# Splitting the expert weights in pieces of 2048 columns, with six landing places instead of nine

## The chip, the cores and the metric

One core of a Trainium2 chip runs the whole program: TensorE (PE; PEld is its weight load), VectorE (DVE), ScalarE (ACT), GpSimd (POOL), and the queue on SyncE (SP) that issues the loads from HBM. The metric is the device time of one execution in microseconds, lower is better.

## The reference

A transformer with two blocks on 256 tokens of width 1024, all in fp32. The first block has a mixer (mLSTM and gMLP), a cross-attention, and a mixture of experts; the second has two layers of a convolution, linear attention and pooling mixer with a gated feed-forward. The part that matters here is the mixture of experts, which comes after a router that gives every token two of 32 experts:

```python
def expert_block(args):
    xb, e = args
    return (jax.nn.silu(xb @ w_gate[e]) * (xb @ w_up[e])) @ w_down[e]
```

With d = 1024 and 512 hidden columns an expert has three matrices of 2 MB each, so 32 experts have 192 MB of weights, all of which are read once.

## The kernel before

**Splits.** A matmul at full precision is made of faster ones: a weight tile `raw` is split in a high part `whi` (a copy on ACT that rounds, line 455) and a low part `wlo` (`raw - whi` on DVE, line 456), and PE multiplies with both. A split of 1024 columns is called a chunk; `wlo` of a chunk needs its `whi`. In the expert stage a chunk feeds four matmuls of 512 columns (lines 968 and 969 for gate and up, 985 and 986 for down), which alternate between `whi` and `wlo`.

**The expert stage.** Experts go in 16 pairs; `up(j)` computes gate and up of pair j from 16 chunks, `down(j)` the down projection from 8. Pairs 13 and 14 are finished late: there is no down between `up(14)` and `up(15)`. Each chunk is a step; small work stands in `plan[step]`, and a generator that yields n goes on n steps later. Of that small work: `features` gathers a pair's tokens (PE, then ACT writes `XT`, line 876), `gate` and `gated` form silu(gate) times up (`z`, `g`; lines 900 to 910), `fold` transposes the result (PE line 925, which reads `g`) and writes `at`, `combine` adds results into the token sums (line 944), and `filters` prepares tables of the second block (lines 1303 to 1325). On PE, ACT and DVE the order is exactly the order in which this code runs (`manual_schedule`), each engine in order.

**Rings and landing places.** Weights of this stage are loaded 1 MB at a time (two chunks) by SP into landing places that are taken in turn: `EARLY` = 2 tiles of their own and seven tiles of the first block that have become free (`PLACES`). `load()` is called after the second chunk of a place is split, and SP issues that load when both parts have been read out of the place it reuses. `whi` has a ring of `NH` = 5 chunks and `wlo` one of `NL` = 4; `weights()` splits ahead:

```python
self.pos += 1
self.ahead(min(self.pos - 1 + NH, self.most))
```

So with chunk n the splits of chunk n+4 stand in the program. Its `whi` reuses the buffer of chunk n-1 and its `wlo` that of chunk n, and ACT or DVE waits until PE has finished there.

**Elsewhere.** Outside of the expert stage the same `whi` and `wlo` rings are filled chunk by chunk (512 KB loads, line 273), in an order that the scheduler chooses. Between the router and the stage stands a branch (`beyond`, a loop for overflowing experts, run zero times), at which all engines meet.

Of the kernel before, what the change touches and what calls it, by code (L numbers as in the profile page):

```python
# [31 lines left out]
P = 128  # L32
D = 1024
# [34 lines left out]
def _cols(v):  # L68
# [15 lines left out]

WHEN = dict(features=((0, 7), (0, 10), (0, 12), (0, 15), (1, 15), (1, 17), (1, 19), (1, 21)), chosen=0,
            weighted=(0, 3, 6, 9), filters=((4, 18), (8, 23)), combine=(3, 5, 7, 9), mask=8, fold=1)

# [163 lines left out]
class Kernel:  # L251
    def __init__(self, nc, tc, ins, out):
        self.nc, self.tc, self.ins, self.out = nc, tc, ins, out
        self.stream, self.loads, self.splits, self.pos, self.streaming = [], 0, 0, 0, False
        self.first_block = True
        self.raws, self.ready = deque(), deque()


# [6 lines left out]
    def weights(self, name, n, parts=None):  # L265

        if self.streaming:
            self.pos += 1
            self.ahead(min(self.pos - 1 + NH, self.most))
            return self.ready.popleft()  # L270
        w = min(1024, self.ins[name].shape[2])
        raw = self.raw(w)
        self.nc.sync.dma_start(raw, self.ins[name][n // 2][:, n % 2 * 1024:][:, :w])
        if self.first_block:
            with self.tc.high_priority(200):
                return self.parts(raw)
        return self.parts(raw, parts)

    def parts(self, raw, parts=None):
        hi, lo = parts or (None, None)  # L280
        hi = self.whi.tile([P, 1024], F32R, name="whi") if hi is None else hi
        lo = self.wlo.tile([P, 1024], F32R, name="wlo") if lo is None else lo
        self.split(hi, lo, raw)
        return hi, lo

    def load(self):

        if self.loads < len(self.stream):
            name, n = self.stream[self.loads]
            if name == "w_v0" and n == 0:  # L290
                self.gains = [self.bcast(g, pool=self.experts, tag="XT", bufs=6) for g in ("g_final", "norm_mix_pre0")]
# [3 lines left out]
            self.raws.append(raw)  # L295
            self.nc.sync.dma_start(raw, self.ins[name][n])
# [82 lines left out]

    def bcast(self, name, row=0, n=D, pool=None, tag="gbc", bufs=None):  # L380
        a = self.ins[name]
        t = (pool or self.gbc).tile([P, n], F32, name="gbc", tag=tag, bufs=bufs)
        self.nc.sync.dma_start(t, bass.AP(tensor=a.tensor, offset=a.offset + row * n, ap=[[0, P], [1, n]]))
        return t
# [113 lines left out]
    def block1(self, outer, moe):  # L498
# [3 lines left out]
        with ExitStack() as ctx:  # L502
# [216 lines left out]
            early = moe.enter_context(tc.tile_pool(name="early", bufs=1, reuse_waits="tile"))  # L719
            self.places = deque([(early, f"early{n}") for n in range(EARLY)] + [(outer, tag) for tag in PLACES])  # L720
            for j in range(PAIRS + 1):
# [3 lines left out]
                for d in DOWN(j):  # L725
                    self.stream.extend(("w_ed", 4 * d + 2 * m + n) for n in range(2) for m in range(2))
            self.most = 2 * len(self.stream) + 2
            self.stream.extend(("w_v0", n) for n in range(2))
# [72 lines left out]
            normed = []  # L801
            self.dense_n(oT, "w_o_x", 0, 8, residual(0))
            self.dense_n(oT, "w_o_x", 1, 8, residual(1, logits), True)
            for t in range(2):
                self.route(a, L[:, t], A[:, t], W[:, t])
# [7 lines left out]
    def moe(self, hh, hl, A, W):  # L813
# [4 lines left out]
        with ExitStack() as ctx:  # L818
# [59 lines left out]

            def weighted(o, t, h):


                if t == h == 0:
                    DT[o] = self.junk.tile([P, 4, S], F32, name="DT", tag="xn", bufs=2)
                Dw = a.tile([P, 2, 2, SLOTS], F32, name="Dw")
                for n in range(2):
                    j = 4 * o + 2 * h + n
                    nc.vector.tensor_scalar(Dw[:, n], self.c["slot"][:, None, :].to_broadcast([P, 2, SLOTS]),
                                            rp[:, t, j:j + 1], wp[:, t, j:j + 1], op0=OP.is_equal, op1=OP.mult)
                yield 4
                ps = self.tp()  # L890
                for n in range(2):
                    nc.tensor.transpose(ps[:, n * P:(n + 1) * P], Dw[:, n].rearrange("p i j -> p (i j)"), self.ident)
                yield 2
                nc.scalar.activation(DT[o][:, 2 * h:2 * h + 2, t * P:(t + 1) * P],
                                     ps[:, :2 * P].rearrange("p (n s) -> p n s", s=P), AF.Copy)

            def gate(j, p):
                yield 3
                z = a.tile([SLOTS, 512], F32, name="z")
                nc.scalar.activation(z, p[SLOTS:], AF.Copy)  # L900
                yield 1
                nc.vector.tensor_add(z, p[:SLOTS], z)
# [5 lines left out]
            def gated(j, p):  # L908
                yield 2
                nc.vector.tensor_mul(G[j], G[j], p)  # L910
# [8 lines left out]
            def fold(j, steps):  # L919
# [12 lines left out]
                yield 1  # L932
                nc.vector.tensor_sub(at[:, :, 1], pt, at[:, :, 0].bitcast(F32))

            def result(j, n, p):
                yield 2
                Y[j, n] = a.tile([P, 512], F32, name="ye", bufs=2)
                nc.scalar.activation(Y[j, n], p, AF.Copy)
# [61 lines left out]
            for k in range(2):  # L1000
                start(features(0, k))
            self.ahead(2)
            go_on()
            for j in range(PAIRS + 1):
# [9 lines left out]
                if j == PAIRS - 1:  # L1014
                    plan[22].append(fold(j, 3))
                if j == 1 or j % 4 == 3 and j < PAIRS - 1:
# [30 lines left out]
            xg = [self.junk.tile([P, D], F32, name="xn", bufs=2) for t in range(2)]  # L1047
            ws = [a.tile([P, 2, 512], F32, name="w", tag="at", bufs=2) for t in range(2)]
            ws = [[w[:, n] for n in range(2)] for w in ws]
# [33 lines left out]
            for t in range(2):  # L1083
                next(combine(PAIRS - 1, t, 1))
            with tc.manual_schedule(engines=engines - {mybir.EngineType.PE}):
                tiles = [chain(half(t, 0), half(t, 1)) for t in range(2)]
                for step in ORDER:
                    if step < 2:
                        next(tiles[step])
                    elif step == 3:  # L1090
                        next(spectra[1])
                    else:
                        self.ahead(self.splits + 1)
            self.streaming = False
            return hT

    def rank(self, a, hh, hl, A, W, rk, mine):
# [31 lines left out]
        self.ahead(2)  # L1129
        self.beyond(a, hh, hl, trips, late)  # L1130
# [227 lines left out]
    def mix(self, l, hT):  # L1358
# [3 lines left out]
        with ExitStack() as ctx:  # L1362
# [75 lines left out]
            nc.sync.dma_start(raw, self.ins[f"w_lr{l}"][0])  # L1438
            wlr = self.whi.tile([P, 1024], F32R, name="whi")
            nc.scalar.activation(wlr, raw, AF.Copy)  # L1440
# [265 lines left out]
```

## Time and profile before

| | us |
|---|---|
| median of 3 runs (lowest, highest) | 1703.29 (1701.62, 1704.55) |
| the profiled execution: its own time | 1706.44 |
| its span, first to last instruction | 1704.6 |
| expert stage in it, first to last matmul of the experts | 262.9 to 801 |

The times of the trace are counted from the start of the span. The span and the time of the profiled execution differ by 1.8 us, which lie around the instructions.

### The profile page before, as it was taken

How to read it: one execution, taken by the hardware profiler on the slowest of the kernel's cores; microseconds unless marked ns; L12 is line 12 of the kernel's file. 1: busy time of each engine (PE TensorE's matmuls, PEld its weight loads, DVE VectorE, ACT ScalarE, POOL GpSimd, SP SyncE). 2: the span in 40 equal slices, each digit the busy share in tenths (PEclk: the TensorE clock that was granted, in tenths of full speed). 3: DMA queues.
4: the chain of work that ended last, by engine and by line, in shares of the span. 5: the costliest groups of instructions: out<-in, count | busy, mean ns of one | idle time of the engine just before them, and what ended most of it. 6: DMA issues, size and time to landing. Idle time of an engine off the chain costs nothing. (4 is left out here: it accounts for less than half of the span.)

```text
span 1704.6 us, 24749 instructions
## 1 busy us (share of the span) xinstructions
PE 1635.3 (96%) x9115; PEld 1380.2 (81%) x9115; DVE 1288.6 (76%) x1702; ACT 1133.9 (67%) x1576; POOL 30.3 (2%) x47
## 2 busy tenths in 40 slices
PE   7999987999999999988999999999999999999998
PEld 6897875777767777766799887999878998789986
DVE  7876566999989999998569667677556886667763
ACT  7765437899878899986667545555445864555552
POOL 1000000000000000000000000000000000000000
PEclk9999998999999999999999999999999999999999
DMA  8546537999999999994775356455756545635561
GB/s 292 199 155 204 191 148 266 352 380 373 381 380 380 402 386 408 416 400 170 253 252 186 128 189 223 143 185 182 238 171 222 202 150 181 214 130 185 183 198 62
DMA packets 94448, 415.92 MB, mean 244 GB/s; under 512 B 12324, under 2 KB 18868, under 8 KB 68468
## 3 DMA queue, kind: packets, MB, share of 16 engines
q1 hardware_dynamic: 89220, 405.91, 65.6%
q0 software_dynamic: 864, 6.29, 1.0%
q10 hardware_dynamic: 4240, 2.10, 0.4%
q8 instruction: 73, 1.20, 0.3%
q14 instruction: 51, 0.42, 0.1%
HBM read 411.12 MB, written 3.15 MB: 243 GB/s over the span
## 5 line engine op out<-in xcount | busy, mean ns | idle before, releaser
L456 DVE TENSOR_TENSOR wlo<-raw,whi 128x1024 fp32r<-128x1024 f32 x709 | 844.3, 1220 | 210.7 <-PE acc L333 80.7
L455 ACT ACTIVATE whi<-raw 128x1024 fp32r<-128x1024 f32 x711 | 728.7, 1055 | 230.6 <-PE acc L334 116.7
L337 PE MATMUL acc<-hl,whi 128*128 128x256 f32 x1024 | 289.9, 283 | 0.0
L338 PE MATMUL acc<-hh,wlo 128*128 128x256 f32 x1024 | 289.9, 283 | 0.0
L336 PE MATMUL acc<-hh,whi 128*128 128x256 f32 x1024 | 289.7, 283 | 0.0
L968 PE MATMUL misc<-whi,XT 128*128 128x512 f32 x512 | 227.5, 444 | 1.1 <-ACT XT L876 1.1
L969 PE MATMUL misc<-wlo,XT 128*128 128x512 f32 x512 | 208.5, 407 | 5.2 <-DVE wlo L456 5.1
L336 PEld LDWEIGHTS acc<-hh,whi 128*128 128x128 f32 x1024 | 196.5, 192 | 0.1
L337 PEld LDWEIGHTS acc<-hl,whi 128*128 128x128 f32 x1024 | 196.5, 192 | 0.0
L338 PEld LDWEIGHTS acc<-hh,wlo 128*128 128x128 f32 x1024 | 196.5, 192 | 0.0
L969 PEld LDWEIGHTS misc<-wlo,XT 128*128 128x128 f32 x512 | 97.9, 191 | 47.7 <-DVE wlo L456 22.4
L968 PEld LDWEIGHTS misc<-whi,XT 128*128 128x128 f32 x512 | 98.1, 192 | 30.4 <-issue 8.9
L332 PE MATMUL acc<-whi,hh 128*128 128x512 f32 x288 | 113.3, 395 | 0.6 <-ACT hh L423 0.5
L333 PE MATMUL acc<-wlo,hh 128*128 128x512 f32 x288 | 113.0, 393 | 0.1
L334 PE MATMUL acc<-whi,hl 128*128 128x512 f32 x288 | 112.4, 391 | 0.0
L985 PE MATMUL misc<-whi,at 128*128 128x512 f32 x256 | 105.8, 413 | 4.3 <-ACT whi L455 2.2
L986 PE MATMUL misc<-wlo,at 128*128 128x512 f32 x256 | 104.1, 407 | 1.7 <-DVE wlo L456 1.7
L944 PE MATMUL acc<-ye,DT 128*128 128x512 f32 x128 | 65.3, 595 | 0.0
L986 PEld LDWEIGHTS misc<-wlo,at 128*128 128x128 f32 x256 | 48.1, 188 | 20.7 <-DVE wlo L456 9.9
L332 PEld LDWEIGHTS acc<-whi,hh 128*128 128x128 f32 x288 | 54.3, 189 | 12.8 <-ACT hh L423 1.2
L334 PEld LDWEIGHTS acc<-whi,hl 128*128 128x128 f32 x288 | 54.2, 188 | 11.6 <-DVE hl L424 0.7
L333 PEld LDWEIGHTS acc<-wlo,hh 128*128 128x128 f32 x288 | 54.4, 189 | 11.3 <-DVE wlo L456 0.5
(466 smaller groups left out, 2724.0 us busy)
## 6 DMA issues: line engine op xcount, KB each, us to landing
raw<-in_w_egu SPq DMA_DIRECT2D x128, 1024.0 KB
raw<-in_w_ed SPq DMA_DIRECT2D x64, 1024.0 KB
raw<-in_w_up SPq DMA_DIRECT2D x80, 512.0 KB
raw<-in_w_gate SPq DMA_DIRECT2D x48, 512.0 KB
raw<-in_w_down SPq DMA_DIRECT2D x44, 512.0 KB
raw<-in_w_qk SPq DMA_DIRECT2D x24, 512.0 KB
raw<-in_w_out SPq DMA_DIRECT2D x24, 512.0 KB
raw<-in_w_br SPq DMA_DIRECT2D x24, 512.0 KB
```

What stands on the lines that cost most here:

```text
L332: mm(out, xh, wh, start=start, stop=False)
L333: mm(out, xh, wl, start=False, stop=False)
L334: mm(out, xl, wh, start=False, stop=stop)
L336: mm(out, wh, xh, start=start, stop=False)
L337: mm(out, wh, xl, start=False, stop=False)
L338: mm(out, wl, xh, start=False, stop=stop)
L455: self.nc.scalar.activation(hi, src, AF.Copy)
L456: self.nc.vector.tensor_sub(lo, src, hi.bitcast(F32))
L968: mm(p, l, wh[:, c], start=s == k == 0, stop=False)
L969: mm(p, l, wl[:, c], start=False, stop=s == 7 and k == 1)
L985: mm(p, l, wh[:, c], start=s == k == 0, stop=False)
L986: mm(p, l, wl[:, c], start=False, stop=s == 3 and k == 1)
```

## The change

The expert stage splits a whole landing place with one instruction on ACT and one on DVE (2048 columns; the last place of the stream in two halves). The rings have four buffers of two chunks each for the high and four for the low part: three `whi` and two `wlo` tiles, and one respectively two tiles of the first block (`hTh`; `hTl`, `mTh`), which are landing places no more. Six places are left. With each even chunk n the split of the place three places further stands in the program. Outside of the stage a tile of the ring holds two chunks (`half`), so a new tile waits for both chunks of the old one. The gains of the last norm are loaded into a landing place, one `at` buffer lies in an `XT` one, the sixth place is loaded earlier, and the step counts of the small work are other ones.

```diff
-NB, NH, NL = 6, 5, 4
-PLACES = ("kT", "qk", "mTl", "y", "hTh", "hTl", "mTh")
+NB, NH, NL = 6, 3, 2
+PLACES = ("kT", "qk", "mTl", "y")
 EARLY = 2
+HIS, LOS = ("whi", "whi", "whi", "hTh"), ("wlo", "wlo", "hTl", "mTh")
-WHEN = dict(features=((0, 7), (0, 10), (0, 12), (0, 15), (1, 15), ...
-            weighted=(0, 3, 6, 9), filters=((4, 18), (8, 23)), ...
+WHEN = dict(features=((0, 9), (0, 11), (0, 13), (0, 15), (1, 15), ...
+            weighted=(0, 2, 4, 6), filters=((5, 19), (13, 23)), ...
...
         if self.streaming:
+            if self.pos % 2 == 0:
+                self.ahead(min(self.pos // 2 + len(HIS), self.pos + 2))
             self.pos += 1
-            self.ahead(min(self.pos - 1 + NH, self.most))
             return self.ready.popleft()
...
+    def half(self, n):
+        if not self.halves[n]:
+            t = (self.whi, self.wlo)[n].tile([P, 2048], F32R, name=("whi", "wlo")[n])
+            self.halves[n] = [t[:, 1024:], t[:, :1024]]
+        return self.halves[n].pop()
...
-        hi = self.whi.tile([P, 1024], F32R, name="whi") if hi is None else hi
-        lo = self.wlo.tile([P, 1024], F32R, name="wlo") if lo is None else lo
+        hi = self.half(0) if hi is None else hi
+        lo = self.half(1) if lo is None else lo
...
     def ahead(self, n):
-        while self.splits < min(n, 2 * len(self.stream)):
-            raw = self.raws[0]
-            self.ready.append(self.parts(raw[:, self.splits % 2 * 1024:][:, :1024]))
-            self.splits += 1
-            if self.splits % 2 == 0:
-                self.raws.popleft()
-                self.load()
+        while self.splits < min(n, len(self.stream) - 2):
+            for _ in self.apart(2048):
+                pass
+    def apart(self, w):
+        raw = self.raws.popleft()
+        self.splits += 1
+        hi, lo = (ring[0][0].tile([P, 2048], F32R, name="part", tag=ring[0][1]) for ring in self.rings)
+        for ring in self.rings:
+            ring.rotate(-1)
+        for a in range(0, 2048, w):
+            c = slice(a, a + w)
+            self.split(hi[:, c], lo[:, c], raw[:, c])
+            self.ready.extend((hi[:, b:b + 1024], lo[:, b:b + 1024]) for b in range(a, a + w, 1024))
+            if a + w < 2048:
+                yield
+        self.load()
...
             self.dense_n(oT, "w_o_x", 0, 8, residual(0))
+            self.load()
             self.dense_n(oT, "w_o_x", 1, 8, residual(1, logits), True)
...
-                yield 1 if q == 0 else 2
+                yield 1
                 nc.scalar.activation(XT[q][k // 2][:, k % 2]...
...
             def gated(j, p):
-                yield 2
+                yield 1
                 nc.vector.tensor_mul(G[j], G[j], p)
...
-                AT[j] = a.tile([P, 4, 2, 2, SLOTS], F32R, name="at", bufs=2)
+                AT[j] = a.tile([P, 4, 2, 2, SLOTS], F32R, name="at", **(dict(tag="XT", bufs=6) if j == PAIRS - 2 else {}))
```

The first place is DVE's order from the `z` of pair 14, in the middle of `up(14)`, to the `at` of that pair in `up(15)`. Before:

```order
L902 TENSOR_TENSOR z<-misc,z 64x512
L456 TENSOR_TENSOR wlo<-raw,whi 128x1024 x6
L910 TENSOR_TENSOR g<-g,misc 128x512
L456 TENSOR_TENSOR wlo<-raw,whi 128x1024 x4
L933 TENSOR_TENSOR at<-tp,at 128x8x64
```

Now (line 481 is the low split, which writes a `part`; the high one is line 480):

```order
L932 TENSOR_TENSOR z<-misc,z 64x512
L481 TENSOR_TENSOR part<-raw,part 128x2048 x2
L940 TENSOR_TENSOR g<-g,misc 128x512
L481 TENSOR_TENSOR part<-raw,part 128x2048 x3
L963 TENSOR_TENSOR at<-tp,at 128x8x64
```

Between `z` and `g` six chunks were split and now four, between `g` and `at` four and now six, and an instruction covers two.

The second place is ACT's order at the start of the stage, where `XT` is the evicted features that the first steps of `up(0)` need. Before:

```order
L876 ACTIVATE XT<-tp 128x2x4x64 x2
L455 ACTIVATE whi<-raw 128x1024 x3
L876 ACTIVATE XT<-tp 128x2x4x64 x2
L455 ACTIVATE whi<-raw 128x1024
L876 ACTIVATE XT<-tp 128x2x4x64 x2
L455 ACTIVATE whi<-raw 128x1024
L876 ACTIVATE XT<-tp 128x2x4x64 x2
```

Now:

```order
L906 ACTIVATE XT<-tp 128x2x4x64 x2
L480 ACTIVATE part<-raw 128x2048
L906 ACTIVATE XT<-tp 128x2x4x64 x4
L480 ACTIVATE part<-raw 128x2048 x2
L906 ACTIVATE XT<-tp 128x2x4x64 x2
```

Four evictions follow the first split instead of two, and the last two stand behind two long splits instead of one short one.

The third place is SP's queue up to the branch (`trips` is the loop's count). Before:

```order
L296 DMA raw<-in_w_egu 128x2048 x2
L273 DMA raw<-in_w_o_x 128x1024 x2
L296 DMA raw<-in_w_egu 128x2048 x6
L1180 TENSOR_LOAD trips
L1184 COMPARE_AND_BRANCH
```

Now:

```order
L310 DMA raw<-in_w_egu 128x2048 x2
L277 DMA raw<-in_w_o_x 128x1024 x3
L310 DMA raw<-in_w_egu 128x2048 x3
L1311 DMA fdft<-in_dft 128x1024
L1314 DMA w_2673<-in_filt_w 128x512
L1211 TENSOR_LOAD trips
```

With two more that stand further ahead in both, ten loads of expert weights were issued before the branch and seven are now.

## Rows read from the trace of the kernel before

**Rows 1.** The page, section 1, busy time, and section 6, loads of expert weights.

```profile
PE 1635.3 (96%) x9115; PEld 1380.2 (81%) x9115; DVE 1288.6 (76%) x1702; ACT 1133.9 (67%) x1576; POOL 30.3 (2%) x47
...
raw<-in_w_egu SPq DMA_DIRECT2D x128, 1024.0 KB
raw<-in_w_ed SPq DMA_DIRECT2D x64, 1024.0 KB
```

**Rows 2.** Busy time by stretch: stretch, length, engines, clock, DMA share, GB/s.

```profile
262.90:801.00 538.10, 516.94 (x2309) 387.75 (x2308) 496.99 (x521) 469.55 (x585) 0.00 (x0) 0.98 0.92 368
...
300.00:350.00 50.00, 48.56 (x232) 37.03 (x231) 46.51 (x52) 43.87 (x59) 0.00 (x0) 1.00 0.96 365
650.00:700.00 50.00, 48.87 (x214) 35.95 (x212) 49.56 (x49) 48.43 (x59) 0.00 (x0) 1.00 1.01 408
700.00:750.00 50.00, 46.53 (x194) 34.56 (x193) 47.05 (x47) 42.90 (x52) 0.00 (x0) 0.97 1.01 420
```

**Rows 3.** Waits in the expert stage: us in total, times, longest.

```profile
DVE wlo L456 <- ACT whi L455: 23.9, 34, 3.7
ACT whi L455 <- PE misc L968: 23.2, 27, 3.9
PEld misc L969 <- DVE wlo L456: 22.4, 49, 1.1
...
PEld misc L986 <- DVE wlo L456: 9.9, 24, 1.1
...
ACT whi L455 <- DMA raw<-in_w_ed: 4.5, 2, 2.2
```

**Rows 4.** Waits of SP's queue in the expert stage.

```profile
SPq L296 <- DVE wlo L456: 369.9, 166, 6.1
```

**Rows 5.** Groups by line and shape, the splits: busy us, mean ns; idle before.

```profile
L456 DVE TENSOR_TENSOR wlo<-raw,whi 128x1024 fp32r<-128x1024 f32 x384 | 448.2, 1217 | 35.3 <-ACT whi L455 23.9 <-issue 6.8 <-PE misc L986 2.9
L455 ACT ACTIVATE whi<-raw 128x1024 fp32r<-128x1024 f32 x384 | 385.7, 1054 | 46.0 <-PE misc L968 23.2 <-issue 11.7 <-PE misc L985 4.6
...
L456 DVE TENSOR_TENSOR Y<-Y 128x512 fp32r<-128x512 f32 x8 | 5.2, 686 | 0.0
...
L455 ACT ACTIVATE Y<-Y 128x512 fp32r<-128x512 f32 x8 | 5.0, 629 | 7.2 <-DVE Y L1579 7.2
```

**Rows 6.** Timeline, splits one behind the other: start, length, count.

```profile
272.29 9.16 DVE L456 TENSOR_TENSOR wlo<-raw,whi 128x1024 fp32r<-128x1024 f32 x8
...
272.18 5.79 ACT L455 ACTIVATE whi<-raw 128x1024 fp32r<-128x1024 f32 x6
```

**Rows 7.** Timeline of PE in the expert stage, two matmuls.

```profile
299.81 0.40 PE L968 MATMUL misc<-whi,XT 128*128 128x512 f32 x1
300.05 0.39 PE L969 MATMUL misc<-wlo,XT 128*128 128x512 f32 x1
```

**Rows 8.** Timeline at the start of `up(15)`.

```profile
738.79 4.63 DVE L456 TENSOR_TENSOR wlo<-raw,whi 128x1024 fp32r<-128x1024 f32 x4 [0.16 <-ACT whi L455]
...
743.34 0.68 DVE L910 TENSOR_TENSOR g<-g,misc 128x512 f32<-128x512 f32 x1
...
744.08 2.07 PE L925 MATMUL tp<-F,g 128*128 128x128 f32 x8 [3.03 <-DVE g L910]
```

**Rows 9.** Timeline of ACT and PE at the start of the stage.

```profile
267.41 1.06 ACT L455 ACTIVATE whi<-raw 128x1024 fp32r<-128x1024 f32 x1
...
271.21 1.09 ACT L876 ACTIVATE XT<-tp 128x512 fp32r<-128x512 f32 x2 [0.35 <-PE tp L873]
...
271.86 0.50 PE L968 MATMUL misc<-whi,XT 128*128 128x512 f32 x1 [0.22 <-ACT XT L876]
```

**Rows 10.** Waits in the second block, 800 us to the end.

```profile
DVE wlo L456 <- PE acc L333: 69.0, 52, 1.6
...
PEld acc L333 <- DVE wlo L456: 0.5, 1, 0.5
```

More of the change, by code (lines that the diff above doesn't have):

```diff
@@ L82 @@
 MEMBERS = [m * PAIRS + j for j in range(PAIRS) for m in range(2)]
-WHEN = dict(features=((0, 7), (0, 10), (0, 12), (0, 15), (1, 15), (1, 17), (1, 19), (1, 21)), chosen=0,
-            weighted=(0, 3, 6, 9), filters=((4, 18), (8, 23)), combine=(3, 5, 7, 9), mask=8, fold=1)
+WHEN = dict(features=((0, 9), (0, 11), (0, 13), (0, 15), (1, 15), (1, 17), (1, 19), (1, 21)), chosen=0,
+            weighted=(0, 2, 4, 6), filters=((5, 19), (13, 23)), combine=(3, 5, 7, 9), mask=8, fold=1)
 DOWN = lambda j: {0: (), PAIRS - 2: (), PAIRS - 1: (PAIRS - 3, PAIRS - 2)}.get(j, (j - 1,))
@@ L256, in __init__ @@
         self.raws, self.ready = deque(), deque()
+        self.halves = [[], []]
     def buffers(self, ctx, name, n, side="left"):
@@ L289, in load @@
             name, n = self.stream[self.loads]
-            if name == "w_v0" and n == 0:
-                self.gains = [self.bcast(g, pool=self.experts, tag="XT", bufs=6) for g in ("g_final", "norm_mix_pre0")]
             self.places.rotate(-1)
@@ L294, in load @@
             raw = pool.tile([P, 2048], F32, name="raw", tag=tag)
-            self.raws.append(raw)
-            self.nc.sync.dma_start(raw, self.ins[name][n])
+            if name == "gains":
+                self.gains = [raw[:, i * D:(i + 1) * D] for i in range(2)]
+                for g, n in zip(self.gains, ("g_final", "norm_mix_pre0")):
+                    self.bcast(n, to=g)
+            else:
+                self.raws.append(raw)
+                self.nc.sync.dma_start(raw, self.ins[name][n])
             self.loads += 1
     def ahead(self, n):
-        while self.splits < min(n, 2 * len(self.stream)):
-            raw = self.raws[0]
-            self.ready.append(self.parts(raw[:, self.splits % 2 * 1024:][:, :1024]))
-            self.splits += 1
-            if self.splits % 2 == 0:
-                self.raws.popleft()
-                self.load()
+        while self.splits < min(n, len(self.stream) - 2):
[14 more added lines that the diff above has]
+        self.load()
     def constants(self, name, pool, w=0):
@@ L719, in block1 @@
             early = moe.enter_context(tc.tile_pool(name="early", bufs=1, reuse_waits="tile"))
-            self.places = deque([(early, f"early{n}") for n in range(EARLY)] + [(outer, tag) for tag in PLACES])
+            self.places = deque([(early, f"early{n}") for n in range(EARLY)]
+                                + [(outer, tag) for tag in PLACES])
+            self.rings = [deque(({"whi": self.whi, "wlo": self.wlo}.get(tag, outer), tag) for tag in tags)
+                          for tags in (HIS, LOS)]
             for j in range(PAIRS + 1):
@@ L726, in block1 @@
                     self.stream.extend(("w_ed", 4 * d + 2 * m + n) for n in range(2) for m in range(2))
-            self.most = 2 * len(self.stream) + 2
+            self.stream.append(("gains", 0))
             self.stream.extend(("w_v0", n) for n in range(2))
@@ L900, in gate @@
                 nc.scalar.activation(z, p[SLOTS:], AF.Copy)
-                yield 1
+                yield 2
                 nc.vector.tensor_add(z, p[:SLOTS], z)
@@ L908, in gated @@
             def gated(j, p):
-                yield 2
+                yield 1
                 nc.vector.tensor_mul(G[j], G[j], p)
@@ L931, in fold @@
                 nc.scalar.activation(at[:, :, 0], pt, AF.Copy)
-                yield 1
+                yield 2
                 nc.vector.tensor_sub(at[:, :, 1], pt, at[:, :, 0].bitcast(F32))
             def result(j, n, p):
-                yield 2
+                yield 3
                 Y[j, n] = a.tile([P, 512], F32, name="ye", bufs=2)
@@ L1001, in moe @@
                 start(features(0, k))
-            self.ahead(2)
+            self.ahead(1)
             go_on()
@@ L1014, in moe @@
                 if j == PAIRS - 1:
-                    plan[22].append(fold(j, 3))
+                    plan[22].append(fold(j, 2))
                 if j == 1 or j % 4 == 3 and j < PAIRS - 1:
@@ L1047, in moe @@
             xg = [self.junk.tile([P, D], F32, name="xn", bufs=2) for t in range(2)]
-            ws = [a.tile([P, 2, 512], F32, name="w", tag="at", bufs=2) for t in range(2)]
+            ws = [a.tile([P, 2, 512], F32, name="w", **kw) for kw in (dict(tag="at"), dict(tag="XT", bufs=6))]
             ws = [[w[:, n] for n in range(2)] for w in ws]
@@ L1084, in moe @@
                 next(combine(PAIRS - 1, t, 1))
+            rest = self.apart(1024)
             with tc.manual_schedule(engines=engines - {mybir.EngineType.PE}):
@@ L1092, in moe @@
                     else:
-                        self.ahead(self.splits + 1)
+                        next(rest, None)
             self.streaming = False
@@ L1128, in rank @@
                                            op0=OP.is_ge, op1=OP.mult)
-        self.ahead(2)
+        self.ahead(1)
         self.beyond(a, hh, hl, trips, late)
@@ L1438, in mix @@
             nc.sync.dma_start(raw, self.ins[f"w_lr{l}"][0])
-            wlr = self.whi.tile([P, 1024], F32R, name="whi")
+            wlr = self.half(0)
             nc.scalar.activation(wlr, raw, AF.Copy)
```

7 lines of the change are left out of this document (4 added, 3 removed).

## Prediction

> **What bounds the kernel now.** The first view is the page: PE is busy for 1635.3 us of the span, so a gain must come from time in which PE waits or is held up [rows 1]. The change touches one stage above all, so the second view is busy time by stretch. The reader should see that the expert stage takes 538.1 us, and that in it PE (516.9), DVE (497.0), ACT (469.6) and the loads (share 0.92) are all nearly full [rows 2]. From 650 to 700 us DVE has 49.6 us of 50. This stage has three or four near bounds, and taking work from one engine pays only down to the next.
>
> Which one ends the waits last? The third view is the waits. PE's weight loads stood for a low part 22.4 + 9.9 = 32.3 us in 73 places [rows 3]; the low part is DVE's. DVE in turn stood 23.9 us for ACT's high part, and ACT 23.2 us for PE to leave a `whi` buffer, in 27 places, up to 3.9 us at once. That is a short ring at work: ACT runs ahead until its five chunks are full, stands, and when PE goes on, DVE has no reserve for its other work. The loads end few waits: ACT waited 4.5 us for one [rows 3], while SP's queue stood 369.9 us, 166 times, for a place that DVE had not yet emptied [rows 4]. So before the change DVE's throughput and the shortness of the rings set the pace, and PE follows in many small steps.
>
> PE's own room in the stage: 538.1 - 516.9 = 21.2 us plainly idle. A matmul is shown for 0.39 us and the next starts 0.24 us after it [rows 7], so a delay under 0.16 us does not show as idle; the 32.3 us of standing weight loads bound what is hidden. PE could thus get back between 21 and 21 + 32 = 53 us, start and end included.
>
> **The change part by part.** The sum is made against the profiled execution (1706.4 us). It stands 3.1 us above the median of 1703.3, and I take the same differences off the median.
>
> *Wide splits.* 384 splits on DVE become 192. One of 1024 columns takes 1217 ns, one of 512 686 ns [rows 5]: 531 ns for 512 columns, so 2048 would take about 1217 + 2 x 531 = 2279 ns. One behind the other they overlap: eight take 9.16 us [rows 6], a step of (9.16 - 1.22)/7 = 1.135 us, 0.082 less than the length. A wide step would be 2.197 us against 2 x 1.135 = 2.270, so 0.073 us saved, 192 x 0.073 = 14 us. If none overlapped it would be 2 x 1.217 - 2.279 = 0.155, 30 us. I take 14, as DVE is busy for 497 of 538 us and its splits mostly stand in rows. ACT likewise: (1054 - 629) for 512 columns gives 1.904 us for a wide one; six in 5.79 us are a step of 0.947; saved 0.097 x 192 = 19 us, on an engine that is less full, so not counted again.
>
> [...]
>
> *Longer rings.* Before, the split with chunk n was that of n+4, and its low part reused the buffer that PE was reading. Now three places (six chunks) are split ahead and the split waits only for the place behind. At PE's pace of 0.24 us, 4 matmuls a chunk, the lead grows from 4 x 0.96 = 3.8 us to 6 x 0.96 = 5.8 us, without any other PE work. At best ACT's 23.2 us and what DVE lost with them come back; at worst nothing, because some of these waits come after PE itself had been held up. I take 9 us, some 40%: DVE would still be 483 of 515 us busy, so little of its idle time is left to use.
>
> *Fold of pair 14.* There `g` stood behind four splits on DVE until 743.34, and PE waited 3.03 us [rows 8]. Two chunks fewer stand ahead of `g` now (first order place), worth 2 x 1.135 = 2.3 us, and `gated` starts a step earlier. I take 3 us off (0 to 4).
>
> *Start of the stage.* The last two `XT` were evicted at 271.21, right behind one split of 1.06 us [rows 9]. Now two wide ones stand there, 2 x 1.8 us, but one of the three short splits ahead of the second `XT` is gone. I add 1.5 us (0 to 3).
>
> *Fewer places, and loads.* Seven loads are issued before the branch instead of ten (third order place). At 538/192 = 2.8 us a place comes round after 6 x 2.8 = 17 us instead of 25. With loads ending 4.5 us of waits I take nothing here; the first rival is what it costs if that cover is gone. The earlier `fdft` load and the gains in a landing place lie beside other work.
>
> *Outside the stage.* A low ring of two tiles with two chunks each makes every second split wait for one chunk more of PE. DVE already stands 69.0 us there in the second block, and PE's weight loads only 0.5 us for a low part [rows 10]: DVE has the reserve. A chunk there is 12 matmuls, some 12 x 0.24 = 2.9 us; if three places lost it, 8 us. I add 2 (0 to 8).
>
> The sum: -14 - 9 - 3 + 1.5 + 2 = -22.5 us, near the lower end of PE's room of 21 to 53. 1706.4 - 22.5 = 1683.9 for such a profiled execution, **1681 us** for the median. Bounds of the terms: all good, -30 - 23 - 4 would be -57, which the loads (below, 40 us at 400 GB/s) cut to about -40, 1663; all poor, -14 + 0 + 0 + 3 + 8 = -3, 1700.
>
> **The rivals.** *The loads become the bound.* For it: their share is 0.96 to 1.01 in the full stretches, so a faster consumer asks for what may not be there. 192 loads of 1.049 MB [rows 1], of which 185 come after the branch, from about 266 us, where the stage's first split would end. At the 420 GB/s of 700 to 750 us [rows 2] a load takes 2.50 us, the last lands at 266 + 462 = 728, and with about 10 us for its split, matmuls and sums the stage ends at 738: no bound. At the 365 GB/s of 300 to 350 us (share 0.96) it takes 2.87 us, the end is 266 + 531 + 10 = 807, 6 us later than now. At the stage's own 368 GB/s at a share of 0.92, which is 400 at a share of 1, it takes 2.62 us and the end is 266 + 485 + 10 = 761, 40 us earlier. So it decides from 387 GB/s down; at 375 the stage ends at 794, 7 us earlier, and the median is 1696. Against it: SP waits for DVE and not the other way round.
>
> [...]
>
> *Small work comes late (slower).* ACT and DVE run in order, and a wide split is one piece of about 2 us. ACT is now tied to PE in every second step: what stands behind the split waits until PE has left the place before, plus the split. If the chain `z`, `g`, `fold` is late in every pair as it was in one [rows 8], 16 x 3.0 = 48 us are lost against 22 won: +26, 1729. It decides from 22.5/16 = 1.4 us a pair. For it: one such wait is there now, and step counts alone keep it off. Against it: `g` has moved ahead, ACT's load falls by 19 us. I would expect some 1715.
>
> *Nothing.* The pace is PE's small steps for other reasons, the 14 us of DVE become idle time and the rings outside cost a few us: 1700 to 1706.
>
> **How the numbers follow.** A measurement tells 0.2% (3.4 us) from no change. The forecast (1664 to 1699) has 0.66, the loads (1690 to 1700) 0.12, nothing 0.08, late small work 0.14. Faster: 0.66 + 0.12 = 0.78; same 0.08; slower 0.14. The range 1660 to 1706 takes in the first three cases and leaves the slower one out; the likeliest one's own range is 1664 to 1699.
>
> **What would show it.** Wide splits: DVE's group of 192 with a mean of 2.28 us and ACT's with 1.90. Rings: ACT's waits for PE fall below 23 us though each may be longer, and weight loads standing for a low part fall from 32 to below 15 us. Fold: no wait of 3 us in `up(15)`. Loads: if waits of ACT or DVE for a DMA grow from 4.5 us to over 15, the first rival is at work. Late work: PE waits for `g`, `XT`, `DT` or `at` over 20 us together. Outside: stretches from 850 us on within 3 us of the present ones. The forecast is wrong if the expert stage is not 15 us or more shorter, or if the gain lies elsewhere.

## The result and the profile after

The changed kernel takes 1716.93 us (median of 4 runs, 1714.75 to 1719.03) against 1702.86 for the kernel before; the ratio is 1.0082, 95% interval 1.0064 to 1.0099. It is some 14 us slower, where 22 us less had been forecast. The profiled execution took 1714.75 us with a span of 1712.6. The page's busy times, which answer to [rows 1], and then busy time over the expert stage, from its first to its last matmul (columns as in [rows 2]):

```profile
PE 1632.9 (95%) x9115; PEld 1384.5 (81%) x9115; DVE 1262.2 (74%) x1509; ACT 1109.4 (65%) x1383; POOL 30.0 (2%) x47
```

```profile
264.10:811.50 547.40, 513.48 (x2309) 393.79 (x2308) 481.63 (x328) 451.29 (x393) 0.00 (x0) 0.98 0.93 366
```

Against [rows 2] the stage starts 1.2 us later and is 9.3 us longer; after it, 901.1 us follow instead of 903.6. Together that is the 8.0 us between the two spans, so the loss that the traces show is in the stage. They show less than the 14 us of the medians: the profiled execution of the kernel before (1706.44 us) was slower than the four runs of its median, that of the changed kernel the fastest of its four. In the stage DVE is busy 15.4 us less and ACT 18.3 us less, as the change was costed; PE's idle time, stretch less busy, went from 21.2 to 33.9 us. The engines that were given less to do also stand more: DVE 65.8 us instead of 41.1.

Where each stands is in the waits of the stage (us in total, times, longest), which answer to [rows 3]:

```profile
DVE part L481 <- ACT part L480: 51.5, 32, 4.6
ACT g L936 <- DVE z L932: 30.9, 14, 4.3
...
PE misc L1015 <- DVE g L940: 14.2, 13, 2.2
...
ACT part L480 <- PE misc L998: 9.7, 16, 1.9
...
PE tp L955 <- DVE g L940: 8.1, 2, 4.1
...
DVE Dw L917 <- PE tp L922: 6.0, 4, 2.9
...
PEld misc L999 <- DVE part L481: 4.0, 7, 1.3
ACT part L480 <- PE misc L1015: 3.9, 4, 1.4
ACT part L480 <- DMA raw<-in_w_egu: 3.2, 5, 1.0
PE misc L998 <- ACT XT L906: 3.1, 3, 2.4
...
PE misc L1015 <- DVE z L932: 2.3, 3, 1.2
PEld misc L1016 <- DVE part L481: 2.0, 9, 0.3
```

Two waits of the kernel before that answer to lines of this list:

```profile
ACT g L906 <- DVE z L902: 7.7, 7, 1.8
...
PE misc L985 <- DVE g L910: 2.0, 6, 0.9
```

The two waits that the longer rings were to cure are cured: weight loads stand 4.0 + 2.0 us for a low part instead of 32.3, ACT 9.7 + 3.9 us for PE instead of 23.2 + 4.6. In their place DVE stands 51.5 us for high parts (23.9 before), and ACT 30.9 us at Silu, which in the kernel before had waited 7.7 us, 7 times. PE's wait for `g` ahead of the down projection went from 2.0 to 14.2 us, nearly all of the 12.7 us by which its idle time grew. One pair shows how these hang together. ACT's timeline (start, length, idle time before and its releaser) in `up(9)`:

```profile
581.09 0.60 ACT L930 ACTIVATE z<-misc 64x512 f32<-64x512 f32 x1
581.60 1.92 ACT L480 ACTIVATE part<-raw 128x2048 fp32r<-128x2048 f32 x1
584.28 1.92 ACT L480 ACTIVATE part<-raw 128x2048 fp32r<-128x2048 f32 x1 [0.76 <-PE misc L998]
588.67 1.28 ACT L936 ACTIVATE g<-z 64x512 f32<-64x512 f32 x2 [2.47 <-DVE z L932]
```

DVE's timeline beside it:

```profile
585.76 2.29 DVE L481 TENSOR_TENSOR part<-raw,part 128x2048 fp32r<-128x2048 f32 x1
587.96 0.68 DVE L932 TENSOR_TENSOR z<-misc,z 64x512 f32<-64x512 f32 x1
588.56 2.28 DVE L481 TENSOR_TENSOR part<-raw,part 128x2048 fp32r<-128x2048 f32 x1
592.33 2.29 DVE L481 TENSOR_TENSOR part<-raw,part 128x2048 fp32r<-128x2048 f32 x1 [1.49 <-ACT part L480]
594.54 0.68 DVE L940 TENSOR_TENSOR g<-g,misc 128x512 f32<-128x512 f32 x1
```

And PE's, a little later:

```profile
595.27 0.50 PE L1015 MATMUL misc<-part,at 128*128 128x512 f32 x1 [0.58 <-DVE g L940]
```

ACT evicts `z` and splits two places, then comes to Silu, which needs `z` with DVE's addition. DVE has the addition behind a wide low split and reaches it late. ACT stands 2.47 us, and with it the next high part; so DVE, done with its reserve, stands 1.49 us for that part; so `g`, behind the split in DVE's order, is late, and PE stands for it in the first matmul of the down projection.

How late the addition comes has two parts. The first is the order. The change also put the addition one step later, in lines that the diff above leaves out:

```diff
                 nc.scalar.activation(z, p[SLOTS:], AF.Copy)
-                yield 1
+                yield 2
                 nc.vector.tensor_add(z, p[:SLOTS], z)
                 yield 2
```

On ACT two wide splits now stand between `z` and Silu; in the trace two take 3.71 us one behind the other. On DVE the addition comes after the low split of the first of them, which starts when its high part is done: 1.9 + 2.2 + 0.7 = 4.8 us. By the splits alone Silu would wait 1.1 us. But ACT has other small work there too, and waits of its own: in the 16 pairs it takes 4.2 to 6.9 us from the start of `z` until it is ready for Silu.

The second part, and the larger one, is how far DVE runs behind ACT. In the pair shown the first high part ends at 583.52. A free DVE would have done the addition 2.88 us later, at 586.4, and ACT was ready for Silu at 588.67 - 2.47 = 586.20: 0.2 us of waiting. But DVE began that low split only at 585.76, 2.24 us after its high part, and with that the wait became 2.47 us. Worked out in this way for all 16 pairs (an estimate from the same timelines), 3.6 of the 30.9 us would be left if DVE were never behind; on the mean it is 1.8 us behind, and the order leaves no margin for it (-0.1 us). In the kernel before, DVE is 1.1 us behind on the mean, and the order leaves 0.7 us. Its `up(9)`, where it just fits, first ACT and then DVE:

```profile
577.07 0.60 ACT L900 ACTIVATE z<-misc 64x512 f32<-64x512 f32 x1
577.57 2.94 ACT L455 ACTIVATE whi<-raw 128x1024 fp32r<-128x1024 f32 x3
580.50 1.28 ACT L906 ACTIVATE g<-z 64x512 f32<-64x512 f32 x2
```

```profile
578.65 1.23 DVE L456 TENSOR_TENSOR wlo<-raw,whi 128x1024 fp32r<-128x1024 f32 x1 [0.34 <-ACT whi L455]
579.79 0.68 DVE L902 TENSOR_TENSOR z<-misc,z 64x512 f32<-64x512 f32 x1
```

DVE's lag in the changed kernel is longest, 3.6 to 3.9 us, in pairs 1, 3, 7 and 11, and 15.0 of the 30.9 us fall on these four. They are the pairs in whose `up` DVE also makes the `Dw` of `weighted` (line 917), where it stands for PE at times. No run takes that work out alone.

### The profile page after: what moved, and what is told of

It is laid out like the page before. It is cut to its first block, busy times and chain, and to the rows that moved or that the text cites. A ratio compares the mean times of both kernels' runs of the same rounds, so it can differ in the third digit from the quotient of the medians.

```text
span 1712.6 us, 23616 instructions
## 1 busy us (share of the span) xinstructions
PE 1632.9 (95%) x9115; PEld 1384.5 (81%) x9115; DVE 1262.2 (74%) x1509; ACT 1109.4 (65%) x1383; POOL 30.0 (2%) x47
## 5 line engine op out<-in xcount | busy, mean ns | idle before, releaser
L481 DVE TENSOR_TENSOR wlo<-raw,whi 128x1024 fp32r<-128x1024 f32 x321 | 382.1, 1219 | 162.6 <-issue 57.6
L481 DVE TENSOR_TENSOR part<-raw,part 128x2048 fp32r<-128x2048 f32 x195 | 437.4, 2274 | 52.4 <-ACT part L480 51.5
L480 ACT ACTIVATE whi<-raw 128x1024 fp32r<-128x1024 f32 x323 | 330.5, 1052 | 192.4 <-PE acc L359 75.5
L480 ACT ACTIVATE part<-raw 128x2048 fp32r<-128x2048 f32 x195 | 366.8, 1906 | 40.5 <-issue 18.8
L998 PE MATMUL misc<-part,XT 128*128 128x512 f32 x512 | 229.4, 448 | 7.6 <-ACT ye L968 4.4
L999 PE MATMUL misc<-part,XT 128*128 128x512 f32 x512 | 205.8, 402 | 1.2 <-DVE part L481 0.8
L998 PEld LDWEIGHTS misc<-part,XT 128*128 128x128 f32 x512 | 98.2, 192 | 40.5 <-issue 9.6
L999 PEld LDWEIGHTS misc<-part,XT 128*128 128x128 f32 x512 | 98.5, 192 | 33.5 <-issue 11.3
L1015 PE MATMUL misc<-part,at 128*128 128x512 f32 x256 | 108.1, 422 | 16.5 <-DVE g L940 14.2
L357 PE MATMUL acc<-whi,hh 128*128 128x512 f32 x272 | 106.3, 392 | 0.3 <-ACT hh L448 0.3
L358 PE MATMUL acc<-wlo,hh 128*128 128x512 f32 x272 | 106.4, 392 | 0.1
L1016 PE MATMUL misc<-part,at 128*128 128x512 f32 x256 | 103.3, 404 | 0.0
L1015 PEld LDWEIGHTS misc<-part,at 128*128 128x128 f32 x256 | 49.0, 191 | 31.4 <-DVE g L940 8.2
```

The costliest lines, as they stand in the source:

```text
L357: mm(out, xh, wh, start=start, stop=False)
L358: mm(out, xh, wl, start=False, stop=False)
L480: self.nc.scalar.activation(hi, src, AF.Copy)
L481: self.nc.vector.tensor_sub(lo, src, hi.bitcast(F32))
L998: mm(p, l, wh[:, c], start=s == k == 0, stop=False)
L999: mm(p, l, wl[:, c], start=False, stop=s == 7 and k == 1)
```

## The experiments

Theory A: instructions twice as wide double the delay in each handoff between engines, and the small chain that goes from ACT to DVE to ACT to DVE no longer fits. Its rivals: the other step counts by themselves, the deeper lead of the rings, the six places. Each ratio is against runs of the kernel before on the same chip.

**Pieces of 1024 in the changed kernel.**

```diff
-            for _ in self.apart(2048):
+            for _ in self.apart(1024):
```

> The changed kernel, with each landing place split by two pairs of instructions of 1024 columns, one directly behind the other, in the same rings, places and step counts. Theory A (the width does the harm: the low part of 2048 columns starts 1.9 us after its high part, and the small work waits behind 2-us pieces): DVE's waits for ACT's high part fall from 51.5 us below 35, ACT's wait for z from 30.9 below 20, PE's plain idle in the expert stage (33.9 us now, 21.2 before the change) back towards 25, the time 1705 to 1712 although the fixed costs of 192 more instructions return. Rivals (the lead of the rings, the step counts or the six places do it): the waits stay within a fifth, and the time is 1717 or up to 14 us more, 1715 to 1731.

1706.78 us, ratio 1.0016 (1.0005 to 1.0026). Waits in its stage:

```profile
ACT g L936 <- DVE z L932: 27.6, 12, 4.2
DVE part L481 <- ACT part L480: 27.2, 28, 3.7
```

The time and DVE's waits came as theory A has them: nearly as many waits for a high part, each some 0.6 as long, 10 us back, and PE's idle time in the stage at 27.5 us. ACT's wait for `z`, expected below 20, hardly fell: by the sum above, an estimate from this run's timelines, the order has its margin of 0.7 us again, but DVE is 2.3 us behind. So the width makes a break in step dear, but something else causes the break.

**Addition and Silu both two steps earlier.**

```diff
-                yield 2
                 nc.vector.tensor_add(z, p[:SLOTS], z)
                 yield 2
                 G[j] = ...
```

> The changed kernel, with DVE's addition that completes z put right behind the copy of z on ACT, so that one wide low split fewer stands ahead of it; everything else is unchanged. If the chain z, add, Silu is where the stage loses its time: ACT's wait for z falls from 30.9 us below 8, DVE's wait for the high part from 51.5 below 35, PE's waits for g from 30 us below 12, the time 1703 to 1710. If that chain only shows a delay that has another cause (lead, places): the wait moves to other lines, and the time stays at 1715 to 1719.

1714.58 us, 1.0066 (1.0049 to 1.0083); ACT's wait for `z` 35.3 us. The edit was not the one that its expectation describes: Silu's count runs on from the addition, so Silu moved along, and the distance between the two in the queues stayed. It shows that the place of the chain as a whole is nearly indifferent.

**Six places in the kernel before.**

```diff
-PLACES = ("kT", "qk", "mTl", "y", "hTh", "hTl", "mTh")
+PLACES = ("kT", "qk", "mTl", "y")
```

> The kernel before, with six landing places (hTh, hTl and mTh are taken out of the list and lie unused), its rings and chunks of 1024 unchanged. My prediction took nothing for fewer places. If that holds: within 3 us of before, SP's queue waits more, ACT's waits for a load stay below 10 us. Rival (the places are a part of the loss): 5 to 12 us slower, ACT's waits for a load over 15 us.

1700.80 us, 0.9986 (0.9973 to 0.9998). No wait of ACT for a load is among the stage's waits. Fewer places cost nothing; why they give 0.1% is not settled.

**The old step counts in the changed kernel.**

```diff
-... features=((0, 9), (0, 11), (0, 13), ... weighted=(0, 2, 4, 6), filters=((5, 19), (13, 23))
+... features=((0, 7), (0, 10), (0, 12), ... weighted=(0, 3, 6, 9), filters=((4, 18), (8, 23))
```

with the yields of `features`, `weighted`, `gate`, `gated`, `fold` and `result` as before.

> The changed kernel, with the step counts of the small work (features, weighted, filters, and the yields of features, gate, gated, at, result) set back to those of before. If the new counts do the harm: 1700 to 1710, with ACT's wait for z near the 7.7 us of before. Theory A (width): the same waits in other places, within 4 us of 1717 or slower, up to 1725, as the counts were made for chunks of 1024.

1732.40 us, 1.0171 (1.0153 to 1.0190): 15 us worse than the change, more than theory A's bound of 1725. ACT's wait for `z` is 10.2 us, yet PE stands 26.0 us for `g` ahead of the down projection, and ACT 45.1 us for PE. The new counts are not the harm as a whole.

**Which handoff: the low part alone in pieces, the high part alone, and a shorter lead.** The first two put several instructions in place of one in `apart`; the third:

```diff
-                self.ahead(min(self.pos // 2 + len(HIS), self.pos + 2))
+                self.ahead(min(self.pos // 2 + len(HIS) - 1, self.pos + 2))
```

> The changed kernel with the high part in one instruction of 2048 columns and the low part in two of 1024, one directly behind the other. With both parts in pieces of 1024 the time fell by 10 us against the changed kernel, and DVE's waits for the high part halved from 51.5 to 27.2 us in as many times. Theory A1 (what costs is the handoff from ACT to DVE: after each restart DVE stands until a whole high part of 2048 is written): nothing is won here, DVE's waits for the high part stay at 45 to 55 us, and the time is 1716 to 1724. Rival A2 (the handoff from DVE to PE: PE gets the first 1024 columns later): PE's weight loads wait less for low parts, and the time is 1704 to 1711.

> The changed kernel with the high part in two instructions of 1024 columns, one directly behind the other, and the low part in one of 2048. DVE still starts only when all of the high part is written. Theory A1 (handoff from ACT to DVE): DVE's waits for the high part stay at 45 to 55 us, the time is 1715 to 1724. Rival A3 (ACT's own granularity: a wide copy holds up the evictions and Silu behind it and waits for a whole place of the ring to be free): the time falls to 1705 to 1711 as with both parts in pieces.

> The changed kernel with the splits one landing place less ahead (with each even chunk the split of the place two further, not three, stands in the program); rings and places unchanged. If the deep lead does the harm (ACT waits for PE in every second step, and what stands behind it too): ACT's waits for PE of 13.6 us go to nearly nothing, and the time falls to 1705 to 1712. Theory A (handoff): the lead is reserve, PE's waits for low parts grow from 6 us above 20, and the time is 1717 to 1735.

Low part in pieces: 1725.93 us, 1.0137 (1.0121 to 1.0152), 2 us above the range of theory A1, DVE's waits for ACT 48.0 us. High part in pieces: 1720.68 us, 1.0105 (1.0089 to 1.0121), 55.1 us. Neither alone gives anything back (the first is even 9 us slower than the change, which is not explained), and PE gains nothing from getting low parts in pieces. Only when both are in pieces, so that DVE may start after 1024 columns, do 10 us return: it is the handoff from ACT to DVE. With the shorter lead 1742.95 us, 1.0233 (1.0219 to 1.0247), 8 us above the range of theory A: PE's weight loads stand 40.6 + 29.2 us for low parts. But DVE also stands 23.6 us, 12 times, for PE at the `Dw` (6.0 us, 4 times, in the change). So the lead is needed with these step counts; with counts made for a shorter one it was not tried.

**The addition two steps earlier, Silu kept.**

```diff
                 nc.scalar.activation(z, p[SLOTS:], AF.Copy)
+                nc.vector.tensor_add(z, p[:SLOTS], z)
                 yield 2
-                nc.vector.tensor_add(z, p[:SLOTS], z)
                 yield 2
```

> The changed kernel with DVE's addition that completes z two steps earlier, and Silu where it was (in the run before with the early addition, Silu moved two steps forward with it, so its distance to the addition in the queues was kept, and ACT's wait for z too, 35 us). Now one wide split fewer stands ahead of the addition while Silu stands behind as many as before. If ACT's waits for z, which stop the high parts and so starve DVE, are a cause: they fall from 30.9 us below 10, DVE's waits for the high part from 51.5 below 35, and the time is 1704 to 1711. If they are only a symptom of DVE being late: the waits go elsewhere and the time stays at 1713 to 1719.

1700.75 us, 0.9986 (0.9975 to 0.9997), 16 us faster than the change. ACT's wait for `z` falls to 6.7 us, DVE's for the high part to 35.7.

**Width, once the chain fits; and the same edit in the kernel before.** The last kernel with `apart(1024)`, and the kernel before with `yield 1` ahead of the addition put behind it.

> The changed kernel with the addition to z two steps earlier and Silu kept (1700.8 us with wide pieces) and, on top, both parts in two pieces of 1024 columns back to back. It tells what the width itself is worth once the chain of z is no longer late. If the wide instruction is a saving on DVE and ACT as my prediction had it (14 us of DVE time, less where it stands idle): 1703 to 1712, DVE busy some 14 us longer in the stage. If the handoff of 2048 columns still costs: 1692 to 1698. If neither matters with PE nearly always busy: within 2 us of 1700.8.

> The kernel before, with the addition to z put directly behind the copy of z, one step earlier, and Silu kept at its step. ACT's waits for z are only 7.7 us there, so if the chain was nearly free of waits in the kernel before: 1698 to 1704, ACT's waits for z below 4. If the addition was late there too and hid behind other waits: 1690 to 1697, as much as the 16 us that the same edit gave in the changed kernel.

1700.05 us, 0.9979 (0.9969 to 0.9989), and 1699.73 us, 0.9985 (0.9976 to 0.9993). With the chain repaired, wide pieces are worth nothing against narrow ones, although the narrow kernel's DVE is busy more: its group of 384 low splits takes 442.8 us where 192 wide ones take 430.1. And the kernel before gains 3 us by the same edit, with ACT's wait for `z` at 1.5 us: the addition was a little late there too.

**The new step counts in the kernel before.**

> The kernel before with the step counts of the changed one (features, weighted, filters and the yields, the addition to z one step later among them). With chunks of 1024 and a lead of four chunks the addition then has one more split ahead of it. If the new counts need the wide splits and longer rings: 1706 to 1720, ACT's waits for z over 20 us. If they are better by themselves: 1695 to 1702.

1725.00 us, 1.0130 (1.0113 to 1.0147). That is 5 us above the upper range. ACT's wait for `z` is 15.7 us, not above 20, and PE stands 22.9 us for low parts. The largest wait that the kernel before does not have at all is this:

```profile
DVE Dw L887 <- PE tp L892: 23.4, 12, 4.0
```

The new counts start the four `weighted` of a pair at steps 0, 2, 4, 6 instead of 0, 3, 6, 9 and transpose a `Dw` seven steps after it is made instead of four, and DVE, in order, stands at a new `Dw` until PE has transposed an older one. The shorter lead above shows the same wait in the changed kernel (23.6 us). No run changes these counts alone. The counts belong to splits and rings: each set is 15 to 22 us worse in the other kernel.

**Silu later: with the addition earlier, and by itself.** The first has the addition directly behind the copy and then `yield 5`; the second is one digit in the changed kernel:

```diff
                 nc.vector.tensor_add(z, p[:SLOTS], z)
-                yield 2
+                yield 3
```

> The changed kernel with the addition to z two steps earlier, and Silu one step later than it was, so that both ends of the chain have moved apart. ACT's remaining waits for z (6.7 us, 6 times) should go to under 2. If ACT's queue matters still: 1696 to 1700, and DVE's waits for the high part fall from 35.7 us. If g is then late for the product with up and for the fold: PE's waits for g (11.8 us, 8 times) grow, 1702 to 1710.

> The changed kernel with Silu one step later and nothing else: one more wide high split stands ahead of it on ACT, the addition stays where it was on DVE. If ACT's standing at Silu (30.9 us, which stops the high parts and starves DVE) is what costs: ACT's waits for z fall below 10, DVE's waits for high parts below 40, the time 1699 to 1706. If the late addition itself costs, through g and the fold: 1712 to 1720.

1696.10 us, 0.9960 (0.9948 to 0.9972), and 1696.92 us, 0.9972 (0.9962 to 0.9982). The digit alone gives back 20 us between the medians, some 19 by the ratios, and the time falls below the range that was expected; it leaves the addition where it was. With the addition early as well nothing more is gained, though no wait of ACT for `z` is left among the stage's waits. Three wide splits, some 5.6 us, now stand between `z` and Silu, against 4.8 us until the addition is done; by the sum over 16 pairs, an estimate of the same kind, the order leaves 2.5 us on the mean, and only pairs 1, 7 and 11 still wait. Waits of the stage with the digit alone:

```profile
DVE part L481 <- ACT part L480: 31.6, 21, 4.6
...
ACT part L480 <- DMA raw<-in_w_egu: 7.6, 15, 0.9
...
ACT g L936 <- DVE z L932: 5.5, 3, 2.1
...
PE misc L1015 <- DVE g L940: 1.6, 3, 0.9
```

Its ACT timeline in the same pair, where Silu no longer waits although the addition comes at 575.49 (ACT also stands 1.49 us for PE there, at an eviction of `filters`):

```profile
568.89 0.59 ACT L930 ACTIVATE z<-misc 64x512 f32<-64x512 f32 x1
569.43 1.92 ACT L480 ACTIVATE part<-raw 128x2048 fp32r<-128x2048 f32 x1
571.92 1.92 ACT L480 ACTIVATE part<-raw 128x2048 fp32r<-128x2048 f32 x1 [0.57 <-PE misc L998]
575.33 0.39 ACT L1350 ACTIVATE fk<-tp 128x256 f32<-128x256 f32 x1 [1.49 <-PE tp L1347]
575.61 0.25 ACT L1352 ACTIVATE fk<-tp 1x128 f32<-1x128 f32 x1
575.77 1.90 ACT L480 ACTIVATE part<-raw 128x2048 fp32r<-128x2048 f32 x1
577.58 1.25 ACT L936 ACTIVATE g<-z 64x512 f32<-64x512 f32 x2
```

PE's wait for `g` ahead of the down projection goes from 14.2 to 1.6 us with it. So the cause is ACT's standing at Silu and not the late addition in itself. The wide pieces set its price: with pieces of 1024 ACT stood nearly as long there (27.6 us), and the kernel was 3 us slower than the one before, not 14.

**The folds too, and the whole repair in the kernel before.** Addition early and Silu late, and the folds that come directly behind another `up`:

```diff
-                    plan[WHEN["fold"]].append(fold(j - 1, 3))
+                    plan[5 if j in (1, PAIRS - 1) else WHEN["fold"]].append(fold(j - 1, 3))
```

> The run with the addition two steps earlier and Silu one step later (1696.1 us), and on top the folds of pairs 0 and 14 four steps later in the up that follows directly, since there g stands on DVE just ahead of the fold and PE waited 2.3 and 3.1 us for it. If these waits are on the path: both vanish, 1690 to 1694. If PE only waits elsewhere then: 1695 to 1698.

> The kernel before with the same three edits: the addition to z directly behind the copy, Silu at the same chunk as in the run above, and the two folds four steps later; its splits of 1024, rings and nine places are kept. If wide splits, longer rings and the rest of the change are worth something by themselves: 1696 to 1702, at least 4 us above the run above. If they are worth nothing because PE itself is the bound: within 2 us of it.

1694.46 us, 0.9959 (0.9944 to 0.9974), and 1695.94 us, 0.9959 (0.9942 to 0.9975). PE's waits for `g` ahead of a fold are gone in both. The folds bring at most 2 us in the medians and nothing in the ratio (0.9960 without them), so that term stays within the noise. Busy time over the stage, first the changed kernel with the three edits:

```profile
263.20:788.40 525.20, 507.86 (x2309) 389.23 (x2308) 481.58 (x328) 452.30 (x393) 0.00 (x0) 0.99 0.96 382
```

and the kernel before with them:

```profile
261.00:790.80 529.80, 513.00 (x2310) 385.21 (x2308) 494.54 (x519) 468.86 (x585) 0.00 (x0) 0.99 0.93 374
```

With the same repair both kernels are 0.4% faster than before, and no difference between them can be told. In the stage the changed one is 4.6 us shorter, but it starts 2.2 us later, and the profiled execution of the other was the slowest of its five runs, so this is no measured difference.

## Why the prediction was wrong, step by step

The step that failed is the price of the small work in every pair: the sum has no term for it beside a gain at one fold and the start of the stage, and the slower rival is set aside because "`g` has moved ahead, ACT's load falls by 19 us". What the runs showed in its place is ACT's standing at Silu, 30.9 us; putting Silu one step later gives back some 19 us. Two terms of the sum were wrong beside it: the 14 us for wide splits are worth nothing that can be measured, and the 9 us for the rings rest on room that PE did not have.

*Lengths of the wide splits: right.* Over the stage DVE's group of 192 has a mean of 2.285 us (forecast 2.279), ACT's 1.914 (1.904):

```profile
L481 DVE TENSOR_TENSOR part<-raw,part 128x2048 fp32r<-128x2048 f32 x192 | 432.8, 2285 | 52.2 <-ACT part L480 51.5
L480 ACT ACTIVATE part<-raw 128x2048 fp32r<-128x2048 f32 x192 | 362.9, 1914 | 38.7 <-issue 18.8 <-PE misc L998 9.7 <-PE misc L1015 3.9
```

*What that is worth: wrong.* The 14 us were taken off the time because "DVE is busy for 497 of 538 us". DVE's busy time fell by them, and the time did not: with the chain repaired, wide and narrow pieces take 1700.8 and 1700.1 us. DVE's busy share did not make it the bound.

*Longer rings: the mechanism right, the 9 us wrong.* Both named waits fell as forecast, and with the new step counts the lead is needed. But the room was counted too large: "21.2 us plainly idle" and 32.3 us hidden in standing weight loads. When these fell to 6 us, PE's busy time in the stage fell only from 516.9 to 513.5, and with the later Silu (5.1 us of standing) to 506.6. Of the 32 us at most 10 were time of PE, and less by a nearer comparison: in the repaired kernel before weight loads still stand 24.7 + 6.6 us for a low part, and PE is busy for 513.0 us (granted clock 0.99 in both).

*The slower rival, given a chance of 0.14, came true.* The place, small work behind wide splits in ACT's and DVE's order, came out. The named sign too: PE's waits for `g` and `XT` in the stage are 14.2 + 8.1 + 3.1 + 0.2 = 25.6 us (10.1 before), over the 20. The size ("some 1715") came out by luck: the rival's own sum, 3.0 us in every pair, gave 1729, and nothing leads from there to 1715. And its first cause is not what the trace shows: ACT is not held longer by PE, its waits for PE halved (27.8 to 13.6 us). What weighed against it was wrong: "`g` has moved ahead, ACT's load falls by 19 us". That looks at the end of the chain. The link that broke is in its middle, from the addition to Silu, and none of the prediction's rows showed that ACT already waited there (7.7 us, 7 times). The order of both engines was at hand, and the sum of 3.7 against 4.8 us could have been worked out from [rows 5, 6] as above. It would have shown that the link has no reserve; how far DVE runs behind ACT, which made most of the wait, is in no row of the prediction.

*Fold of pair 14: wrong.* PE stood there 4.07 us instead of 3.03 [rows 8] (the view ends after five of the eight matmuls):

```profile
753.81 1.40 PE L955 MATMUL tp<-F,g 128*128 128x128 f32 x5 [4.07 <-DVE g L940]
```

Fewer chunks stood ahead of `g` in DVE's order, but the split just ahead of it itself waited 1.08 us for ACT's high part, behind Silu.

*Start of the stage: right.* `up(0)` takes 25.8 us against 24.3, and PE stands 2.4 us there for the last `XT`. *Outside: nothing lost.* The rest after the stage is 2.5 us shorter where 2 us more were taken; the kernel before with six places has 901.7 us there, nearly the same, so no gain is read from it.

*Loads: right that they are not the bound.* ACT's waits for loads are 3.2 us, and 9.1 us in the kernel with the later Silu, whose stage takes 382 GB/s on the mean:

```profile
263.30:788.70 525.40, 506.62 (x2309) 390.85 (x2308) 480.82 (x327) 451.81 (x393) 0.00 (x0) 0.99 0.96 382
```

The loads come near to being the bound, though: with the folds moved too, ACT's waits for loads are 8.3 + 4.8 + 2.6 = 15.7 us, just over the 15 that the prediction named as the sign of its first rival, while in the repaired kernel before, with its nine places, no wait of ACT for a load is among the waits of 3.3 us and more.

What stays open: how the 22 us that the new counts cost the kernel before divide between the `Dw` and other waits; whether the change is worth the 1.5 us by which the medians of the two repaired kernels differ; and whether the loads now hold back the repaired changed kernel, which no run with other places tests.

## What to carry to other kernels

Where engines hand small work to each other between long instructions in fixed order, write down for each link what stands on either queue between giver and taker, and sum it: the taker's queue must hold longer work than the giver's, by as much as the giver's engine runs behind. The sum alone is not enough; read that lag from the trace. Making instructions wider changes both sums, and by unequal amounts, since the consumer of a wide instruction started only at its end (in the changed kernel no wide low part began earlier than 0.03 us after the end of its high part; in `up(9)` the one that had waited 1.49 us began at 592.33, its high part having run from 590.40 to 592.30); here one step count was worth some 19 us, more than the whole change. And an engine that is busy for 92% of a stage is not shown to be its bound: take work from it in the sum only as far as the engine that waits for it shows idle time.

## What the runs showed of the hardware that was not expected

Weight loads that stand for 32 us need not cost PE as much: when 26 us of this standing were gone in the changed kernel, PE was busy in the stage for only 3.5 us less (516.9 to 513.5). And the DMA engines of a single core moved 382 GB/s, nearly all of it weights, over a whole stage of 525 us in the kernel with the later Silu, against 368 in the stage of the kernel before [rows 2].
